# A hybrid decoder trunk on one core: constants, small tiles and pools padded so that large SBUF tiles lie at multiples of 256 bytes

## The chip, the cores and the metric

One core of one Trainium2 chip runs the kernel. The metric is device microseconds of one execution. The engines' names are those of the profile: PE (matrix multiply; PEld is its loading of weights), DVE, ACT, POOL (elementwise engines) and SP (which issues most DMAs). SBUF is the on-chip memory from which PE reads; an address in it is a byte offset that is the same in all 128 partitions.

## What is computed

A layer of three sub-layers on a residual stream x of 1024 tokens by 1024 features, all in float32:

```python
h = rms_norm(x, g[0]);  p = h @ w_in_first
y_conv = conformer_conv(p[..., :2 * D_CONV], ...)      # 31-tap causal convolution, layer norm, silu
y_rwkv, _ = rwkv7_mix(p[..., 2 * D_CONV:], ...)        # a recurrence over 1024 tokens, 8 heads of 64
x = x + rms_norm(concat([y_conv, y_rwkv]) @ w_out, g[1])
y = memory_cross_attention(rms_norm(x, g[2]), mem_n, wq, wkv, wo)   # 256 memory tokens, 4 heads
x = x + rms_norm(y, g[3])
y = swiglu(rms_norm(x, g[4]), w_gu, w_down)            # 1024 -> 2 x 2816 -> 1024
x = x + rms_norm(y, g[5])
```

## The kernel before

The 1024 tokens go in two blocks of 512. Every float32 product of a large matrix is made of three products of rounded parts (`mm3`, lines 192 to 196): each operand is split into a high part (`whi`, `ahi`, `fhi`: a rounding copy on ACT, line 166) and a low part (`wlo`, `alo`, `flo`: the difference, on DVE or POOL, line 167), and PE computes high by high (L194), high by low (L195) and low by high (L196). Weights come by DMA in tiles of 128 x 1024 floats (`wload`, lines 169 to 182), four raw buffers deep, two split buffers deep, four in the last feed-forward (pool `we`).

There are two forms. In `feat` (lines 198 to 206, output tile `psf`) a piece of 128 x 128 weights is the stationary operand and an activation tile of 128 x 512 is the moving one. In `tokmajor` (lines 208 to 227, output `pst`) 128 x 128 of an activation is stationary and 128 x 512 of weights is moving. Either way a weight tile gives 24 matmuls of 512 columns; the moving operand of one is 2048 contiguous bytes in each partition, the stationary one 512. By the code the 512-column matmuls of L194 to L196 are:

- input projection: 20 weight tiles of block 0 (activations in pool `a0`) and 22 of block 1 (pool `a1`), `feat`;
- output projection and the two products of attention, for each block 3 x 192, `tokmajor` (stationary in `a2` for block 0, `a3` for block 1);
- feed-forward of each block: gate and up, 44 weight tiles, `feat` (activations in `a2`, `a3`); down, 528 matmuls, `tokmajor` (stationary in `f0`, `f1`).

The order of work is fixed in `run` (line 946 on), partly by hand with generators that weave a side task into a main one: projections of block 0, preparation of the recurrence (`rwkv_prep`), triangular inverses (`rwkv_inverse`, lines 585 to 645, long on POOL), the chain over chunks (`rwkv_chain`) woven with the memory products and the convolution (`conv`, 31 taps a channel group on DVE); then output, attention, and the feed-forward of block 0 woven with the recurrence of block 1; at the end the feed-forward of block 1 alone. The framework's planner puts instructions on the engines' queues and lays out the tiles.

Where tiles lie: the planner rounds each buffer up to 32 bytes and stacks pools from both ends. The left stack starts at byte 16512 with the constants (`cols` 840 bytes, `lora_hi`, and so on), then pool `w` at 34880, `small` at 67648, and from 68480 the pools that are opened and closed on the left. The right stack starts at 229344 and grows downwards. Taken modulo 256, this puts the tiles of the constants at 224 or 64, all of `w` (`wraw`, `whi`, `wlo`) at 64, every large tile of a left pool (`a2`, `f0`, `f1`, `we`, `ya`) at 128, and every large tile of a right pool (`a0`, `a1`, `a3`, `mk`, `kv`) at 224. Buffers of 2080 bytes (tag `p2` of `rwkv_prep`) and 2168 bytes (`hin`) lie at changing multiples of 32.

Of the kernel before, what the change touches and what calls it, by code (L numbers as in the profile page):

```python
# [9 lines left out]
F32 = mybir.dt.float32  # L10
F32R = mybir.dt.float32r
# [6 lines left out]
P = 128  # L18
# [3 lines left out]
TB = 512  # L22
# [3 lines left out]
HP = 4  # L26
HEADS = 8
HD = 64
CH = 64
NCH = TB // CH  # L30
GW = 128
CONVW = 31
# [17 lines left out]
NCOLS = _o  # L50
# [19 lines left out]
class Trunk:  # L70
    def __init__(self, ctx, tc, x, mem, cols, lora, gpost, w_in, w_out, wqT, wkv, wo, w_gu, w_down, out):
        self.ctx, self.tc, self.nc = ctx, tc, tc.nc
        self.x, self.mem, self.out = x, mem, out
        self.w_in, self.w_out, self.wqT, self.wkv = w_in, w_out, wqT, wkv
        self.wo, self.w_gu, self.w_down = wo, w_gu, w_down
        self.gpost = gpost
        nc = self.nc
        pool = lambda name, bufs=1, **kw: ctx.enter_context(tc.tile_pool(name=name, bufs=bufs, **kw))
        self.cp = cp = pool("const")
        self.wp = self.wq = pool("w", 2)  # L80
        self.wbufs = 2
        self.sp = pool("small", 4)
        self.pd = pool("pd", 4, space=PSUM)
        self.pr = pool("pr", 3, space=PSUM)
        self.pn = pool("pn", 1, space=PSUM)
        dr = pool("dram", 1, space=DRAM)

        self.cols = cp.tile([P, NCOLS], F32, name="cols")
        nc.sync.dma_start(out=self.cols, in_=cols)
        self.lora = lora  # L90
        self.lora_hi = cp.tile([P, 3, DR], F32R, name="lora_hi")
        self.lora_lo = cp.tile([P, 2, DR], F32R, name="lora_lo")

        self.ident = cp.tile([P, P], F32, name="ident")
        make_identity(nc, self.ident)
        self.ones = cp.tile([P, P], F32, name="ones")
        nc.gpsimd.memset(self.ones, 1.0)
        self.mhalf = cp.tile([P, 1], F32, name="mhalf")
        nc.gpsimd.memset(self.mhalf, -0.5)
        self.carry = cp.tile([P, 14], F32, name="carry")  # L100
        nc.gpsimd.memset(self.carry, 0.0)
        self.smask = cp.tile([P, NCH, CH], F32, name="smask")
        nc.gpsimd.memset(self.smask, 1.0)
        nc.gpsimd.memset(self.smask[:, :, 0:1], 0.0)

        m = self.gmask = cp.tile([P, 2, 2 * CH], F32, name="gmask")
        nc.gpsimd.memset(m, 1.0)
        for r in (0, 1):
            rows = m[r * 64:(r + 1) * 64]
            for g in (0, 1):  # L110
                nc.gpsimd.affine_select(out=rows[:, g, 0:64], in_=rows[:, g, 0:64], pattern=[[1, 64]],
                                        compare_op=ALU.is_gt, fill=0.0, base=0, channel_multiplier=-1)
                nc.gpsimd.affine_select(out=rows[:, g, 64:128], in_=rows[:, g, 64:128], pattern=[[1, 64]],
                                        compare_op=ALU.is_ge, fill=0.0, base=0, channel_multiplier=-1)
            nc.vector.tensor_scalar(rows[:, r, 0:64], rows[:, r, 0:64], -1.0, None, op0=ALU.mult)


        def derive(name, n, src, mul, add):
            t = cp.tile([P, n], F32, name=name)
            nc.vector.tensor_scalar(t, src, mul, add, op0=ALU.mult, op1=ALU.add)  # L120
            return t
        col = self.col
        self.omu = derive("omu", 14, col("mu"), -1.0, 1.0)
        self.w0h = derive("w0h", 4, col("w0"), 0.5, 0.0)
        self.a0h = derive("a0h", 4, col("a0"), 0.5, 0.0)
        self.kah = derive("kah", 4, col("k_a"), 0.5, 0.0)
        self.kam = derive("kam", 4, col("k_a"), -0.5, 1.0)
        self.cwh = col("conv_w")
        nc.vector.tensor_scalar(self.cwh, self.cwh, 0.5, None, op0=ALU.mult)
        self.lgh = derive("lgh", 4, col("ln_g"), 0.5, 0.0)  # L130
        self.lbh = derive("lbh", 4, col("ln_b"), 0.5, 0.0)


        self.pool_share = self.share = 0.0
        self.state = cp.tile([P, HP, HD], F32, tag="state", bufs=2, name="state0")
        nc.gpsimd.memset(self.state, 0.0)
        self.blk = cp.tile([P, P], F32R, name="blk")
        nc.vector.tensor_copy(out=self.blk, in_=self.state[:, 0:2, :].rearrange("p h v -> p (h v)"))
        for i in (0, 64):
            nc.vector.tensor_copy(out=self.blk[i:i + 64, i:i + 64], in_=self.ones[i:i + 64, 0:64])  # L140

        self.hd = dr.tile([DR, CONVW - 1 + SEQ], F32, name="hd")
        self.pdr = dr.tile([14 * P, SEQ], F32, name="pdr")
        self.yd = dr.tile([D, SEQ], F32, name="yd")
        self.qd = dr.tile([DR, SEQ // CH, CH], F32, name="qd")
        self.amd = dr.tile([SEQ // CH, P, HEADS, 2 * CH], F32, name="amd")
        self.btd = dr.tile([SEQ // CH, P, HP, 2, HD], F32, name="btd")
        self.vtd = dr.tile([SEQ, DR], F32, name="vtd")
        self.bvd = dr.tile([DR, SEQ], F32, name="bvd")
        self.gnd = dr.tile([DR, SEQ], F32, name="gnd")  # L150
        self.gd = dr.tile([D, XH * MEM], F32, name="gd")
        self.vwd = dr.tile([XH * MEM, D], F32, name="vwd")
        self.x1d = dr.tile([SEQ, D], F32, name="x1d")
        self.x2d = dr.tile([SEQ, D], F32, name="x2d")
        NM = NCH * HEADS
        self.sc1 = [dr.tile([NM, CH, CH], F32, name=f"sc1_{i}") for i in range(NB)]
        self.sc2 = [dr.tile([2 * NM, 32, 32], F32, name=f"sc2_{i}") for i in range(NB)]
        self.sc3 = [dr.tile([NM, 32, 32], F32, name=f"sc3_{i}") for i in range(NB)]

    def col(self, name, i=None, n=1):  # L160
        a, b = COLS[name]
        return self.cols[:, a:b] if i is None else self.cols[:, a + i:a + i + n]
# [173 lines left out]
    def conv_taps(self, b, pool, acc):  # L336
        nc = self.nc
        t0 = b * TB
        for j in CONV_ORDER:
            h = pool.tile([P, TB + CONVW - 1], F32, tag="hin", bufs=2, name="hin")  # L340
            nc.sync.dma_start(out=h, in_=self.hd[j * P:(j + 1) * P, t0:t0 + TB + CONVW - 1])
            a = acc[:, j, :]
            w = lambda k: self.cwh[:, j * CONVW + k:j * CONVW + k + 1]
            nc.scalar.activation(out=a, in_=h[:, 0:TB], func=AF.Identity, scale=w(0), bias=self.col("conv_b", j))
            for k in range(1, CONVW):
                if j == CONV_POOL:
                    p = pool.tile([P, TB], F32, tag="t", bufs=2, name="tap")
                    nc.scalar.activation(out=p, in_=h[:, k:k + TB], func=AF.Copy, scale=w(k))  # L348
                    nc.gpsimd.tensor_tensor(out=a, in0=a, in1=p, op=ALU.add)  # L349
                else:  # L350
                    nc.vector.scalar_tensor_tensor(out=a, in0=h[:, k:k + TB], scalar=w(k), in1=a,  # L351
                                                   op0=ALU.mult, op1=ALU.add)
                if k % 6 == 0:
                    yield 4.0
# [62 lines left out]
    def rwkv_prep(self, b, pool):  # L417

        nc = self.nc
# [3 lines left out]
        half = (slice(0, 64), slice(64, 128))  # L423

        def flat2(name):
            t = pool.tile([P, NCH * (CH + 1)], F32, tag="p2", bufs=8, name=name)
            return t[:, 0:TB]

        def load(i, name):
            t = flat2(name)  # L430
            nc.sync.dma_start(out=t, in_=self.pdr[i * P:(i + 1) * P, t0:t0 + TB])
            return t
# [42 lines left out]
        def decays(hp):  # L475
# [4 lines left out]
            nc.vector.tensor_scalar(L, L, 1.0, None, op0=ALU.add)  # L480
            cs = flat2("cs")
            nc.vector.tensor_tensor_scan(cs, flat(self.smask), L, 0.0, op0=ALU.mult, op1=ALU.add)
            Dx = pool.tile([P, NCH, CH + 1], F32, tag="p2", bufs=8, name="Dx")
            nc.gpsimd.memset(Dx[:, :, 0:1], 1.0)
            nc.scalar.activation(out=Dx[:, :, 1:CH + 1], in_=c3(cs), func=AF.Exp, scale=-0.5 * DECAY)
            nc.scalar.activation(out=L, in_=cs, func=AF.Exp, scale=0.5 * DECAY)
# [463 lines left out]
    def run(self):  # L950
        tc = self.tc
        L, R = "left", "right"
        opened = {}

        def push(name, side):
            opened[name] = tc.tile_pool(name=name, bufs=1, side=side, reuse_waits="tile")
            return opened[name].__enter__()

        def pop(*names):
            for n in names:  # L960
                opened.pop(n).__exit__(None, None, None)
# [4 lines left out]
        self.credit = 0.0  # L966
        conv_cols, mix_cols = (4, 0, 6, 2), (20, 12, 8, 16, 14, 10, 18)

        a1 = push("a1", R)
        ev = push("ev", R)  # L970
        mk = push("mk", R)
# [79 lines left out]
        a3 = push("a3", R)  # L1051
        y1 = push("y1", R)
# [17 lines left out]
        pop("xe")  # L1070
        pop("we")
        pop("f1")
        pop("y1", "a3")


@with_exitstack
# [51 lines left out]
```

## Time and profile before

| | us |
|---|---|
| median of 3 runs (1662.28 to 1664.07) | 1663.06 |
| the profiled execution, whole | 1665.11 |
| its span, first to last instruction | 1663.4 |
| PE busy / DVE / ACT / POOL in the span | 1562.1 / 1055.0 / 722.0 / 368.7 |

PE is busy nearly all the time. Its matmuls are pipelined: the end of one is modelled, so the durations of single matmuls overlap, and the pace is read from starts, as the length of a stretch without waits divided by the weight loads in it, one for each matmul.

### The profile page before, as it was taken

Reading aid. Unit: us, or ns where it says so; the run is one execution under the profiler, and the core shown is the slowest. Engines: PE = TensorE matmul, PEld = TensorE weight load, DVE = VectorE, ACT = ScalarE, POOL = GpSimd, SP = SyncE. Lnnn points to the kernel's source line nnn. Section 1 sums busy time; section 2 is a strip of 40 time slices with the busy share of each in tenths; the row PEclk is TensorE's granted clock in tenths of the full one; section 3 lists DMA queues with packets and bytes.
Section 4 is the critical chain, followed back from the end, with each engine's and each line's share of the span. In section 5 each row is a group of like instructions: output and inputs, shape, how many; then the busy total and the mean of one; then the engine's idle time right before and its main releaser. Section 6 shows DMA issues by size and latency. Waiting matters only on the chain.

```text
span 1663.4 us, 22818 instructions
## 1 busy us (share of the span) xinstructions
PE 1562.1 (94%) x8688; PEld 1257.0 (76%) x8688; DVE 1055.0 (63%) x1501; ACT 722.0 (43%) x1122; POOL 368.7 (22%) x344
## 2 busy tenths in 40 slices
PE   7999866879999999999979889999999999999997
PEld 6777855767787888777757667777887788888886
DVE  5677698997545546768789996636537624343435
ACT  5654335867434434664224556524435232222222
POOL 1032390740000001022561730012113211111111
PEclk9999976889999999999999899999999999999999
DMA  6576967466636336457844335445236532323221
GB/s 206 166 223 190 283 203 220 127 196 216 234 117 203 95 100 192 139 165 210 252 119 141 96 114 161 157 126 204 87 91 229 214 102 89 102 89 101 89 89 51
DMA packets 175644, 257.37 MB, mean 155 GB/s; under 512 B 68912, under 2 KB 110000, under 8 KB 175536
## 3 DMA queue, kind: packets, MB, share of 16 engines
q1 hardware_dynamic: 174576, 255.08, 49.4%
q8 instruction: 68, 1.11, 0.3%
q10 hardware_dynamic: 960, 0.85, 0.2%
q14 instruction: 40, 0.33, 0.1%
HBM read 196.58 MB, written 59.31 MB: 154 GB/s over the span
## 4 chain that ended last, share of the span: by engine, by line
PE 46%; DVE 4%; POOL 4%; issue 2%; DMA 1%; ACT 0%; SPq 0%; POOLq 0%; DVEq 0%; ACTq 0%
PE psf L196 8%; PE psf L195 7%; PE psf L194 7%; PE pst L194 7%; PE pst L195 7%; PE pst L196 7%; DVE acc L351 2%; POOL Tt L617 1%; POOL tm L616 1%; PE psg L523 1%; DVE wlo L167 1%; DMA At<-sc 0%; PE pstr L274 0%; DMA btd<-bt 0%; POOL rstd L234 0%
## 5 line engine op out<-in xcount | busy, mean ns | idle before, releaser
L166 ACT CAST whi<-wraw 128x1024 fp32r<-128x1024 f32 x256 | 267.5, 1047 | 556.8 <-PE psf L195 222.7
L196 PE MATMUL psf<-ahi,wlo 128*128 128x512 f32 (+1 forms) x1200 | 468.7, 391 | 24.6 <-DVE wlo L167 23.5
L194 PE MATMUL psf<-ahi,whi 128*128 128x512 f32 (+1 forms) x1200 | 465.3, 389 | 9.6 <-ACT whi L166 9.4
L195 PE MATMUL psf<-alo,whi 128*128 128x512 f32 (+1 forms) x1200 | 465.1, 388 | 0.0
L167 DVE TENSOR_TENSOR wlo<-wraw,whi 128x1024 fp32r<-128x1024 f32 x223 | 284.7, 1278 | 268.4 <-ACT whi L166 266.7
L196 PEld LDWEIGHTS psf<-ahi,wlo 128*128 128x128 f32 x1200 | 232.3, 194 | 77.0 <-DVE wlo L167 29.2
L194 PEld LDWEIGHTS psf<-ahi,whi 128*128 128x128 f32 x1200 | 232.8, 194 | 58.8 <-ACT whi L166 11.8
L195 PEld LDWEIGHTS psf<-alo,whi 128*128 128x128 f32 x1200 | 232.9, 194 | 48.0 <-issue 1.2
L167 POOL TENSOR_TENSOR wlo<-wraw,whi 128x1024 fp32r<-128x1024 f32 x33 | 79.7, 2414 | 566.1 <-ACT whi L166 508.0
L351 DVE SCALAR_TENSOR_TENSOR acc<-hin,cols,acc 128x512 f32<-128x512 f32 x180 | 165.0, 945 | 0.7
L195 PE MATMUL pst<-wlo,ahi 128*128 128x512 f32 x384 | 152.2, 396 | 0.9 <-POOL wlo L167 0.9
L196 PE MATMUL pst<-whi,alo 128*128 128x512 f32 x384 | 150.5, 397 | 0.0
L194 PE MATMUL pst<-whi,ahi 128*128 128x512 f32 x384 | 137.3, 399 | 2.7 <-ACT ahi L277 2.1
L195 PE MATMUL pst<-wlo,fhi 128*128 128x512 f32 x352 | 138.8, 395 | 0.0
L196 PE MATMUL pst<-whi,flo 128*128 128x512 f32 x352 | 135.3, 393 | 0.0
L194 PE MATMUL pst<-whi,fhi 128*128 128x512 f32 x352 | 135.0, 396 | 0.0
L234 POOL TENSOR_TENSOR rstd<-rstd,mhalf 128x1 f32<-128x1 f32 x50 | 34.1, 689 | 394.1 <-DVE rstd L233 385.6
L349 POOL TENSOR_TENSOR acc<-acc,tap 128x512 f32<-128x512 f32 x60 | 97.1, 1618 | 87.5 <-ACT tap L348 84.1
L916 DVE TENSOR_TENSOR ya<-pst,ya 128x512 f32<-128x512 f32 x80 | 54.2, 686 | 53.5 <-PE pst L196 53.4
L194 PEld LDWEIGHTS pst<-whi,ahi 128*128 128x128 f32 x384 | 71.7, 188 | 20.1 <-ACT ahi L277 2.6
L195 PEld LDWEIGHTS pst<-wlo,ahi 128*128 128x128 f32 x384 | 72.1, 188 | 18.2 <-POOL wlo L167 1.2
L196 PEld LDWEIGHTS pst<-whi,alo 128*128 128x128 f32 x384 | 71.8, 188 | 16.6
(241 smaller groups left out, 2004.0 us busy)
## 6 DMA issues: line engine op xcount, KB each, us to landing
wraw<-in_w_gu_dram SPq DMA_DIRECT2D x88, 512.0 KB, 3.7
wraw<-in_w_in_dram SPq DMA_DIRECT2D x44, 512.0 KB, 4.5
wraw<-in_w_down_dram SPq DMA_DIRECT2D x44, 512.0 KB, 3.6
wraw<-in_wkv_dram SPq DMA_DIRECT2D x16, 512.0 KB, 5.4
am<-amd SPq DMA_DIRECT2D x16, 512.0 KB, 5.5
wraw<-in_w_out_dram SPq DMA_DIRECT2D x16, 512.0 KB, 4.1
wraw<-gd SPq DMA_DIRECT2D x16, 512.0 KB, 4.0
wraw<-vwd SPq DMA_DIRECT2D x16, 512.0 KB, 3.4
```

What stands on the lines that cost most here:

```text
L166: self.nc.scalar.copy(out=hi, in_=src)
L167: (eng or self.nc.vector).tensor_tensor(out=lo, in0=src, in1=hi.bitcast(F32), op=ALU.subtract)
L194: mm(ps, w[0], x[0], start=start, stop=False)
L195: mm(ps, w[0], x[1], start=False, stop=False)
L196: mm(ps, w[1], x[0], start=False, stop=stop)
L234: nc.gpsimd.tensor_tensor(r, r, self.mhalf, op=ALU.pow)
L349: nc.gpsimd.tensor_tensor(out=a, in0=a, in1=p, op=ALU.add)
L351: nc.vector.scalar_tensor_tensor(out=a, in0=h[:, k:k + TB], scalar=w(k), in1=a, op0=ALU.mult, op1=ALU.add)
L523: nc.tensor.matmul(pg[g][:, i, :], bk[half[g], c + i, :], aq[half[g], :, c + i, :], start=True, stop=True)
L616: eng.tensor_tensor(out=w, in0=a, in1=c, op=ALU.mult)
L617: eng.tensor_tensor(out=u, in0=u, in1=w, op=ALU.add)
L916: nc.vector.tensor_tensor(out=y, in0=ps, in1=y, op=ALU.add)
```

## The change

It alters where tiles lie and nothing that is computed. `cols` becomes 224 columns wide (896 bytes) of which 210 are used. The constants `state` and `blk` are made earlier, ahead of the small constants, `mhalf` and `carry` later, and a `pad` of 40 floats is added behind them. A tile `line` of 48 floats is added to the pool `small`, and a pool `edge` with one tile of 56 floats (224 bytes) is opened first on the right. Each of the three new tiles is set to zero once by POOL. `hin` and the buffers `p2` become 576 floats (2304 bytes) wide, of which the same columns as before are used.

```diff
+        nc.gpsimd.memset(self.sp.tile([P, 48], F32, tag="line", bufs=1, name="line"), 0.0)
...
-        self.cols = cp.tile([P, NCOLS], F32, name="cols")
+        self.cols = cp.tile([P, 224], F32, name="cols")[:, 0:NCOLS]
...
-        self.mhalf = cp.tile([P, 1], F32, name="mhalf")
-        nc.gpsimd.memset(self.mhalf, -0.5)
-        self.carry = cp.tile([P, 14], F32, name="carry")
-        nc.gpsimd.memset(self.carry, 0.0)
...
+        self.state = cp.tile([P, HP, HD], F32, tag="state", bufs=2, name="state0")
+        nc.gpsimd.memset(self.state, 0.0)
+        self.blk = cp.tile([P, P], F32R, name="blk")
+        nc.vector.tensor_copy(out=self.blk, in_=self.state[:, 0:2, :].rearrange("p h v -> p (h v)"))
+        for i in (0, 64):
+            nc.vector.tensor_copy(out=self.blk[i:i + 64, i:i + 64], in_=self.ones[i:i + 64, 0:64])
+        self.mhalf = cp.tile([P, 1], F32, name="mhalf")
+        nc.gpsimd.memset(self.mhalf, -0.5)
+        self.carry = cp.tile([P, 14], F32, name="carry")
+        nc.gpsimd.memset(self.carry, 0.0)
+        pad = cp.tile([P, 40], F32, name="pad")
+        nc.gpsimd.memset(pad, 0.0)
...
-            h = pool.tile([P, TB + CONVW - 1], F32, tag="hin", bufs=2, name="hin")
+            h = pool.tile([P, 576], F32, tag="hin", bufs=2, name="hin")[:, 0:TB + CONVW - 1]
...
-            t = pool.tile([P, NCH * (CH + 1)], F32, tag="p2", bufs=8, name=name)
+            t = pool.tile([P, 576], F32, tag="p2", bufs=8, name=name)
...
-            Dx = pool.tile([P, NCH, CH + 1], F32, tag="p2", bufs=8, name="Dx")
+            Dx = pool.tile([P, 576], F32, tag="p2", bufs=8, name="Dx")[:, 0:NCH * (CH + 1)].rearrange("p (c t) -> p c t", c=NCH)
...
+        edge = push("edge", R).tile([P, 56], F32, name="edge")
+        self.nc.gpsimd.memset(edge, 0.0)
...
-        pop("y1", "a3")
+        pop("y1", "a3", "edge")
```

## Rows read from the trace of the kernel before

**Rows 1.** The page: each engine's busy time, share of the span, instructions
```profile
PE 1562.1 (94%) x8688; PEld 1257.0 (76%) x8688; DVE 1055.0 (63%) x1501; ACT 722.0 (43%) x1122; POOL 368.7 (22%) x344
```

**Rows 2.** Windows: bounds, length, busy (x) of each engine, clock, DMA
```profile
200.00:300.00 100.00, 67.39 (x688) 56.66 (x686) 87.12 (x134) 46.10 (x79) 54.11 (x63) 0.74 0.70 220
300.00:400.00 100.00, 87.25 (x776) 74.64 (x777) 91.30 (x107) 68.78 (x111) 41.98 (x26) 0.90 0.59 189
400.00:500.00 100.00, 100.00 (x493) 79.72 (x493) 55.62 (x83) 49.15 (x74) 1.93 (x3) 1.00 0.52 169
...
900.00:1000.00 100.00, 87.01 (x598) 67.47 (x593) 93.50 (x105) 54.86 (x83) 49.30 (x30) 0.91 0.39 117
...
1100.00:1200.00 100.00, 99.16 (x451) 80.13 (x450) 50.07 (x84) 40.06 (x77) 17.03 (x13) 1.00 0.41 135
...
1500.00:1600.00 100.00, 100.00 (x434) 81.12 (x434) 39.88 (x45) 25.37 (x32) 12.01 (x5) 1.00 0.30 92
```

**Rows 3.** PE's waits, longest in total first: who, for whom, us, times, longest
```profile
PE psf L196 <- DVE wlo L167: 23.5, 13, 3.7
PE psvw L194 <- ACT whi L166: 12.1, 3, 5.8
...
PE psq L689 <- DVE Sn L706: 5.1, 4, 2.5
...
PE psv L577 <- DMA v<-pdr: 0.8, 1, 0.8
```

**Rows 4.** Windows without a wait, by place of operands; columns as in rows 2
```profile
42.06:56.58 14.52, 14.52 (x63) 11.68 (x62) 10.29 (x20) 9.00 (x15) 0.00 (x0) 1.00 0.68 201
...
692.45:712.14 19.69, 19.69 (x87) 16.15 (x86) 19.16 (x26) 10.17 (x16) 1.92 (x3) 1.00 0.42 109
1477.14:1521.95 44.81, 44.81 (x193) 36.04 (x192) 18.05 (x17) 11.94 (x16) 4.81 (x2) 1.00 0.35 106
450.36:494.46 44.10, 44.10 (x190) 35.53 (x189) 18.01 (x29) 15.05 (x26) 0.55 (x1) 1.00 0.43 140
1083.33:1127.43 44.10, 44.10 (x190) 35.48 (x189) 14.37 (x22) 12.04 (x21) 5.37 (x3) 1.00 0.39 119
1521.95:1543.75 21.80, 21.80 (x97) 18.02 (x96) 9.71 (x12) 4.73 (x5) 2.41 (x1) 1.00 0.25 79
```

**Rows 5.** Windows: matmuls of 256 columns at full clock, of 512 at half clock
```profile
362.82:368.04 5.22, 5.22 (x45) 5.20 (x44) 5.16 (x9) 2.71 (x4) 0.28 (x1) 1.00 0.75 223
256.08:261.62 5.54, 5.54 (x15) 4.29 (x13) 3.20 (x5) 0.99 (x2) 0.00 (x0) 0.51 1.09 260
```

**Rows 6.** Groups by line and shape: count, busy, mean ns, idle before
```profile
L167 DVE TENSOR_TENSOR wlo<-wraw,whi 128x1024 fp32r<-128x1024 f32 x223 | 284.7, 1278 | 268.4 <-ACT whi L166 266.7 <-ACT yq L691 1.0 <-DMA wraw<-in_w_in_dram 0.3
L166 ACT CAST whi<-wraw 128x1024 fp32r<-128x1024 f32 x256 | 267.5, 1047 | 556.8 <-PE psf L195 222.7 <-PE pst L196 193.7 <-issue 120.6
...
L499 DVE SCALAR_TENSOR_TENSOR ry<-cs,ry 128x512 f32<-128x512 f32 x8 | 5.5, 683 | 0.1
```

**Rows 7.** The same view: matmuls of 512 columns
```profile
L194 PE MATMUL psf<-ahi,whi 128*128 128x512 f32 x1040 | 414.8, 400 | 6.7 <-ACT whi L166 6.7
...
L194 PE MATMUL pst<-whi,ahi 128*128 128x512 f32 x384 | 137.3, 399 | 2.7 <-ACT ahi L277 2.1 <-DVE ya L916 0.5
...
L194 PE MATMUL pst<-whi,fhi 128*128 128x512 f32 x352 | 135.0, 396 | 0.0
```

**Rows 8.** Timeline of the start: start, us, engine, line, what
```profile
1.12 0.11 POOL L101 MEMSET carry<- 128x14 f32 x1
...
2.22 0.31 POOL L136 MEMSET state<- 128x256 f32 x1
...
6.20 0.15 DVE L233 TENSOR_SCALAR rstd<-ss 128x1 f32<-128x1 f32 x1 [1.66 <-ACT junk L248]
6.51 0.55 POOL L234 TENSOR_TENSOR rstd<-rstd,mhalf 128x1 f32<-128x1 f32 x1 [2.18 <-DVE rstd L233]
```

**Rows 9.** The chain that ended last, in order of time
```profile
803.55 7.01 DMA At<-sc
```

More of the change, by code (lines that the diff above doesn't have):

```diff
@@ L134, in __init__ @@
         self.pool_share = self.share = 0.0
[L135 to L140, printed above, removed]
         self.hd = dr.tile([DR, CONVW - 1 + SEQ], F32, name="hd")
```

## Prediction

> **What bounds the kernel now.** I read the page's first section, then stretches of 100 us, then PE's waits. PE is busy for 94% of the span, DVE for 63% [rows 1]. From 400 to 700 us and from 1100 to 1600 us PE is full or within 3% of it at full clock, with DVE at 39 to 61 us of 100 (eight stretches, three of them shown); only between 200 and 400 us and between 800 and 1000 us does PE idle, drop to half clock and meet DVE at 87 to 93 us of 100 [rows 2]. Its waits are few: the largest is 23.5 us in 13 pieces for `wlo` from DVE, and for a DMA 0.8 us is the longest entry [rows 3]. So the end is set by the pace of PE's own matmuls. The duration in a row of groups (400 ns) is no pace, since ends are modelled. The pace is read from stretches in which nothing waits: length divided by the weight loads in it.
>
> **What the pace depends on.** Addresses are not in the trace. They follow from the stacks of tiles as described above, and I give them as the remainder modulo 256 of moving, then stationary operand. The six stretches of 512-column matmuls [rows 4], in their order:
> - `a0` moving, `w` stationary, (224, 64): 14.52 / 62 = 234.2 ns (`a1`, later, lies the same)
> - `a2`, `w`, (128, 64): 19.69 / 86 = 229.0
> - `a3`, `we`, (224, 128): 44.81 / 192 = 233.4
> - `w`, `a2`, (64, 128): 44.10 / 189 = 233.3
> - `w`, `a3`, (64, 224): 44.10 / 189 = 233.3
> - `we`, `f1`, (128, 128): 21.80 / 96 = 227.1
>
> The comparison is close to an experiment. The first three run the same code (`feat`) and differ in where the operands lie; the last three run the same code (`tokmajor`). A moving operand at 128 costs 5 to 6 ns less than one at 64 or 224, and between these two there is no difference; a stationary one at 128 is worth 1 or 2 ns more. It isn't load from other engines: in the 229.0 stretch DVE is busy 19.16 of 19.69 us, and in the 233.4 stretch 18.05 of 44.81.
> At half clock 13 matmuls at (64, 224) take 5.54 us, 426 ns each, and half of that is 213 [rows 5]: there the 512 columns alone set the pace, at one column a cycle of 1.2 GHz. At full clock 256 columns at (224, 64) take 5.22 / 44 = 118.6 ns [rows 5]; twice that less 234.2 leaves 3.0 ns that don't grow with columns. So without any loss per column a matmul would take 213.3 + 3.0 = 216.3 ns, and the rest, 17.9 ns at (224, 64) and 10.8 at (128, 128), grows with the bytes that are streamed and depends on the address.
>
> **Part 1, matmul operands.** The sum of sizes after the change: constants end at 35072 instead of 34880, `w` at 67840, `small` at 68864, and the right stack begins at 229120. All four are multiples of 256, and so is the size of every large buffer, so every operand of L194 to L196 goes to (0, 0). The code has 5328 such matmuls of 512 columns, three times 1040 + 384 + 352 [rows 7]. By class: 1008 at 234.2, 1056 at 229.0, 1056 at 233.4, 1104 at 233.3 (all of block 0's `tokmajor`), 576 at 233.3, 528 at 227.1.
> No operand of the trace is at 0, so the new pace has to be bounded. From above by the nearest row, 227.1: 7.2 + 2.0 + 6.7 + 6.8 + 3.6 + 0 = 26.2 us saved. From below by 216.3: another 10.8 x 5328 = 57.5 us. Past the upper end lies 234, if 0 were as bad as 64 (rival 2). I take 224.4. It is halfway between the nearest row and the middle of the two bounds (221.7): going from 64 to 128 took off 6 to 7 of 17.9 ns, and a further step of that kind down to 0 is as likely as none. That saves 26.2 + 2.7 x 5328 = 40.6 us.
> Not all reaches the end. By the starts in the timeline, 93% of these matmuls follow the one before at full clock and within 250 ns; the others run at half clock or behind a wait and gain nothing. Some 11% of the 93% lie in 300 to 400 and 800 to 1000 us, where DVE and POOL's inverses are late next; there I count half. 40.6 x 0.88 = 35.7 us. The 672 matmuls of 256 columns (by the code: the first panel and the memory products) gain half as much each, 4.9 ns, 3.3 us, and lie where PE is not the bound for about half their time: 1.5 us. Sum 37.2 us.
>
> **Part 2, elementwise engines.** Nothing. L499 reads `cs` at 0, 32, 64, 96, 160 and 192 in its eight instances and `ry` at 128 and 224; its mean is 683 ns for 512 columns, and a weight split takes 1278 ns for 1024, at 64. The ACT split takes 1047 ns over 256 instances, at 64 in `w` and at 128 in `we` [rows 6]. Even a gain would be hidden: ACT and DVE prepare a weight tile in 1.05 and 1.28 us while PE spends 24 x 0.23 = 5.6 us on one.
>
> **Part 3, what is added and moved.** Three POOL memsets of 40 to 56 columns cost between 0.11 us (14 columns) and 0.31 us (256 columns) [rows 8], say 0.13 each. POOL has been idle for 2.18 us when the first `rstd` comes, and that waits for ACT's sum by way of DVE [rows 8]. Cost 0; 0.4 us without that cover. Queued behind them are POOL's constants, which the first projections don't need. The three `blk` copies go ahead of DVE's small constants; DVE then still has most of the 1.66 us before its first `rstd` [rows 8]. Memsetting `state` earlier in the program can't hold up the one DMA on ACT's queue that reads it; if the planner put it behind POOL's masks instead, which end at 6.51 - 2.18 = 4.33 us, ACT would start up to 2 us later. I take 0, since it now runs at 2.22 us, in front of them, and its place in the program only moves forward.
> The larger `p2` buffers make `rwkv_prep` 1792 bytes bigger. It still ends at 136448 below `a0` at 136960, so no pool waits for another that it didn't wait for; on the left, `Tt` of the inverse now also covers the old `ry`. Its memset then waits for readers that finish before the 7.01 us load of `At`, which the same loop needs [rows 9]. Cost 0. DMA counts and sizes stay.
> The planner may place a few instructions differently. PE's largest single waits are 3.7 to 5.8 us [rows 3], so I allow 6 us either way for that.
>
> **Total.** 1663.1 - 37.2 = 1625.9 against the median. Against the profiled execution's 1665.1 it is 1628; that one lies 2 us above the median, and the difference carries over.
>
> **Rivals.**
> 1. All of the loss per column goes. Pace 216.3: (26.2 + 57.5) x 0.88 + 3.0 = 76.7 us, time 1586. For it: the half-clock row shows that columns alone can set the pace. Against it: the step to 128 removed only a third of the loss. The Trainium skill, "TensorE: Matmul & The Clock Gate", section "Back-to-back issue gap", gives a gap of N/2.4 + 2.5 ns, 216 ns at 512 columns, whatever the address. No stretch in this trace reaches it; by that figure 1586 would be what full alignment gives back.
> 2. Slower: 0 behaves like 64 and 224, and 128 was the good place, for instance because both operands then start on the same phase. It decides as soon as (0, 0) costs over 232 ns, today's average. At 234.2 the classes at (128, 64) and (128, 128) lose 5.2 x 1056 + 7.1 x 528 = 9.2 us, the others 2.4 us; x 0.88 = 10 us, time 1673. For it: cost is not monotonic in the remainder (224 is as bad as 64). Against: 64 and 224 share that they are no multiples of 128, and 0 is one.
> 3. Nothing changes, 1663: alignment beyond the 32 bytes that every tile has doesn't count, and the differences in pace come from the stage. The Trainium skill, "SBUF — State Buffer", section "Specifications (TRN2)", names lines of 16 bytes as what access is sensitive to; by that rule all these tiles are equal already. The trace disagrees with it for PE: 227.1 against 233.3 ns in the same code.
> 4. PE gets faster but the end doesn't follow: waits for `wlo` (23.5 us now) grow, or a changed order adds stalls, so that under 15 us are left. Time 1650 to 1660. Against: in the eight full stretches DVE has 40 us of 100 to spare [rows 2].
>
> **How the numbers follow.** Forecast (pace 221.7 to 227.1, time 1612 to 1639) 0.70; rival 1 0.12; rival 2 0.07; rival 3 0.05; rival 4 0.06. Range 1586 to 1656: it takes in the forecast with the planner's 6 us, the near half of rival 1 and the near half of rival 4, and leaves out 0.06 below and 0.15 above. About 0.2% (3.3 us) is what a measurement of this kernel can tell from no change. Faster: 0.70 + 0.12 + 0.05 of rival 4 = 0.87; the same: 0.05 (rival 3) + 0.01 of rival 4 = 0.06; slower: 0.07 (rival 2).
>
> **What would show it.** The feed-forward of block 1 from 1300 us on is the test: its `feat` stretches should fall from 233.4 ns and its `tokmajor` stretches from 227.1 to one and the same pace. At 227 only the row is confirmed and the time is near 1639; at 222, 1612; at 216, rival 1; at 233 or more, rival 2. At half clock 426 ns should stay. DVE and ACT means should not move. I am wrong if the pace falls and PE's waits grow by as much.

## The result and the profile after

| | before | after |
|---|---|---|
| median, us (lowest to highest, 4 runs each) | 1662.67 (1661.02 to 1664.07) | 1641.54 (1637.86 to 1643.87) |
| the profiled execution, its span | 1665.11, 1663.4 | 1639.46, 1637.7 |

The ratio is 0.9871 with a 95% interval of 0.9847 to 0.9895: 21 us less, where 37 were forecast (1626, range 1586 to 1656). The profiled executions lie 2 us above the one median and 2 us below the other, so between the traces 25.7 us are to be found.

The page of after, first section (busy us, share of the span, instructions):

```profile
PE 1537.0 (94%) x8688; PEld 1256.5 (77%) x8688; DVE 1056.9 (65%) x1501; ACT 721.7 (44%) x1122; POOL 369.3 (23%) x347
```

Against [rows 1] PE lost 25.1 us of busy time; the other engines moved by less than 2 us. The three instructions more are POOL's memsets. Apart from these and the constants at the start, which moved on DVE and POOL as in the diff, every engine issues the same instructions in the same order. The tiles lie where the sum of sizes put them: each large one at a multiple of 256.

Windows of after: the six stretches of [rows 4] in the same order, then two that answer to [rows 5], 256 columns at full clock and 512 at half clock (bounds, length, busy (x) of PE, PEld, DVE, ACT, POOL, clock, DMA share, GB/s):

```profile
42.16:56.25 14.09, 14.09 (x63) 11.64 (x62) 10.12 (x18) 9.10 (x15) 0.00 (x0) 1.00 0.69 213
680.15:699.70 19.55, 19.55 (x87) 16.14 (x86) 19.01 (x25) 10.03 (x15) 1.91 (x3) 1.00 0.36 108
1454.88:1498.41 43.53, 43.53 (x193) 36.04 (x193) 18.03 (x17) 11.95 (x15) 4.79 (x2) 1.00 0.35 109
443.54:486.43 42.89, 42.89 (x190) 35.44 (x189) 17.97 (x29) 15.11 (x26) 0.55 (x1) 1.00 0.44 144
1068.87:1111.76 42.89, 42.89 (x190) 35.47 (x189) 14.35 (x22) 12.08 (x21) 5.33 (x3) 1.00 0.39 123
1498.41:1520.17 21.76, 21.76 (x97) 18.02 (x96) 9.71 (x12) 4.73 (x5) 2.39 (x1) 1.00 0.27 81
356.73:361.97 5.24, 5.24 (x45) 5.20 (x44) 5.18 (x9) 2.72 (x4) 0.73 (x1) 1.00 0.75 231
252.18:254.31 2.13, 2.13 (x7) 1.65 (x5) 2.13 (x4) 0.00 (x0) 0.00 (x0) 0.50 1.17 190
```

Length over the matmuls that start in it (62, 86, 192, 189, 189, 96; the third window also counts a load that runs over its edge): 227.3, 227.3, 226.7, 226.9, 226.9 and 226.7 ns. The six paces have become one. The 256-column stretch gives 5.24 / 44 = 119.1 ns (118.6 in [rows 5]): no gain. At half clock it is 2.13 / 5 = 426 ns, as before. Over the some 5,080 matmuls of 512 columns that follow the one before at full clock, the mean from start to start fell from 232.1 to 227.35 ns; that is 24 us, nearly all of the difference.

The same stretches show when it was gained. Their starts moved by 0 (42 us), 6.8 (450), 12.3 (692), 14.5 (1083), 22.3 (1477) and 23.5 us (1522), and the end by 25.7. Between 692 and 1083 us, where block 1's recurrence runs beside the feed-forward of block 0, only 2.2 us came. There was little to gain there: by their starts the 512-column matmuls of this stretch lost 3.1 us, since most are of the class at (128, 64), which stood at 229.0 already.

PE's waits of after (who, for whom, us, times, longest), then three groups (count, busy, mean ns, idle before), then the start of POOL and DVE (start, us, engine, line, what); line numbers are five higher than before from the constants on:

```profile
PE psf L201 <- DVE wlo L172: 25.1, 15, 4.1
PE psvw L199 <- ACT whi L171: 11.7, 3, 6.0
...
PE psq L694 <- DVE Sn L711: 5.3, 4, 2.5
```

```profile
L172 DVE TENSOR_TENSOR wlo<-wraw,whi 128x1024 fp32r<-128x1024 f32 x223 | 285.9, 1283 | 253.4 <-ACT whi L171 251.9 <-ACT yq L696 0.6 <-DMA wraw<-in_w_in_dram 0.3
L171 ACT CAST whi<-wraw 128x1024 fp32r<-128x1024 f32 x256 | 268.0, 1049 | 533.8 <-PE psf L200 182.6 <-PE pst L201 182.1 <-issue 153.7
...
L504 DVE SCALAR_TENSOR_TENSOR ry<-cs,ry 128x512 f32<-128x512 f32 x8 | 5.5, 683 | 0.1
```

```profile
0.80 0.14 POOL L83 MEMSET line<- 128x48 f32 x1 [0.29 <-POOLq L1123]
...
2.54 0.13 POOL L128 MEMSET pad<- 128x40 f32 x1
2.61 0.14 POOL L975 MEMSET edge<- 128x56 f32 x1
...
6.20 0.15 DVE L238 TENSOR_SCALAR rstd<-ss 128x1 f32<-128x1 f32 x1 [1.51 <-ACT junk L253]
6.50 0.55 POOL L239 TENSOR_TENSOR rstd<-rstd,mhalf 128x1 f32<-128x1 f32 x1 [1.93 <-DVE rstd L238]
```

The waits of [rows 3] stand nearly as they were (`wlo` 23.5 to 25.1 us). The splits and the in-place product of [rows 6] take what they took. The added memsets come out of POOL's idle time, and the first `rstd` starts at 6.20 us as in [rows 8].

### The profile page after: what moved, and what is told of

Same layout as the page of the kernel before. It is cut to its first block, busy times and chain, and to the rows that moved or that the text cites. A ratio compares the mean times of both kernels' runs of the same rounds, so it can differ in the third digit from the quotient of the medians.

```text
span 1637.7 us, 22825 instructions
## 1 busy us (share of the span) xinstructions
PE 1537.0 (94%) x8688; PEld 1256.5 (77%) x8688; DVE 1056.9 (65%) x1501; ACT 721.7 (44%) x1122; POOL 369.3 (23%) x347
## 4 chain that ended last, share of the span: by engine, by line
PE 44%; DVE 5%; POOL 4%; issue 2%; DMA 1%; ACT 1%; SPq 0%; POOLq 0%; DVEq 0%; ACTq 0%
PE psf L201 7%; PE psf L199 7%; PE psf L200 7%; PE pst L199 6%; PE pst L200 6%; PE pst L201 6%; DVE acc L356 2%; POOL tm L621 1%; POOL Tt L622 1%; DVE wlo L172 1%; PE psg L528 1%; DMA At<-sc 0%; DVE ya L921 0%; POOL rstd L239 0%; POOL wlo L172 0%
## 5 line engine op out<-in xcount | busy, mean ns | idle before, releaser
L171 ACT CAST whi<-wraw 128x1024 fp32r<-128x1024 f32 x256 | 268.0, 1049 | 533.8 <-PE psf L200 182.6
L201 PE MATMUL psf<-ahi,wlo 128*128 128x512 f32 (+1 forms) x1200 | 462.6, 386 | 26.2 <-DVE wlo L172 25.1
L200 PE MATMUL psf<-alo,whi 128*128 128x512 f32 (+1 forms) x1200 | 460.3, 384 | 0.0
L172 DVE TENSOR_TENSOR wlo<-wraw,whi 128x1024 fp32r<-128x1024 f32 x223 | 285.9, 1283 | 253.4 <-ACT whi L171 251.9
L201 PEld LDWEIGHTS psf<-ahi,wlo 128*128 128x128 f32 x1200 | 231.5, 193 | 74.7 <-DVE wlo L172 30.3
L199 PEld LDWEIGHTS psf<-ahi,whi 128*128 128x128 f32 x1200 | 231.7, 193 | 53.0 <-ACT whi L171 10.0
L200 PEld LDWEIGHTS psf<-alo,whi 128*128 128x128 f32 x1200 | 231.8, 193 | 42.7 <-issue 1.2
L201 PE MATMUL pst<-whi,alo 128*128 128x512 f32 x384 | 148.4, 391 | 0.0
L201 PE MATMUL pst<-whi,flo 128*128 128x512 f32 x352 | 134.3, 390 | 0.0
L354 POOL TENSOR_TENSOR acc<-acc,tap 128x512 f32<-128x512 f32 x60 | 99.4, 1656 | 85.6 <-ACT tap L353 82.0
L201 PEld LDWEIGHTS pst<-whi,alo 128*128 128x128 f32 x384 | 71.8, 188 | 14.5
```

Source lines behind the costliest of these rows:

```text
L171: self.nc.scalar.copy(out=hi, in_=src)
L172: (eng or self.nc.vector).tensor_tensor(out=lo, in0=src, in1=hi.bitcast(F32), op=ALU.subtract)
L199: mm(ps, w[0], x[0], start=start, stop=False)
L200: mm(ps, w[0], x[1], start=False, stop=False)
L201: mm(ps, w[1], x[0], start=False, stop=stop)
```

## The experiments

What is left to ask is why the pace fell, since that decides what another kernel should do. Three theories come first. A is the prediction's: the place of the moving operand counts, and multiples of 128 are the good ones. B: it has to be a multiple of 256. C: only the place of the moving operand relative to the stationary one counts, modulo 256, and equal places are the best. The six rows of before fit C as well as A: moving less stationary is 160, 64, 96, 192, 96 and 0, and the paces are 234.2, 229.0, 233.4, 233.3, 233.3 and 227.1. Places are given as (moving, stationary) modulo 256.

**All tiles at 128, all tiles at 64.** From after, both pads altered alike:

```diff
-        pad = cp.tile([P, 40], F32, name="pad")
+        pad = cp.tile([P, 72], F32, name="pad")      # all128; 56 in all64
...
-        edge = push("edge", R).tile([P, 56], F32, name="edge")
+        edge = push("edge", R).tile([P, 88], F32, name="edge")      # all128; 40 in all64
```

> The changed kernel with both stacks shifted so that every large tile lies at 128 modulo 256 (constants stay at 0). Theory A (what counts is a multiple of 128): pace of the 512-column matmuls 227 ns in every stretch, time within 5 us of the changed kernel, about 1641. Theory B (256 itself counts, and a part of the gain comes from it): pace 229 or more, time 1648 or more. Theory C (what counts is that both operands start at the same place modulo 256): 227 ns, 1641, as A.

> The changed kernel with both stacks shifted so that every large tile lies at 64 modulo 256. Theory A (multiples of 128): pace 233 to 235 ns everywhere, 7 ns over the changed kernel; 7.3 x 5328 x 0.88 = 34 us more, about 1675, which is 10 us above the kernel before, where a third of the operands lay at 128. Theory C (same place for both): 227 ns, about 1641. A line of 16 bytes: no difference, 1641.

Measured: all128 1642.87 us (1641.02 to 1646.9), ratio 0.9877 [0.9859, 0.9894]; all64 1646.51 us (1646.4 to 1647.85), 0.9898 [0.9881, 0.9914]. Windows of all64, `a3` over `we`, `w` over `a2`, `we` over `f1`:

```profile
1461.94:1505.47 43.53, 43.53 (x193) 36.06 (x192) 18.03 (x17) 11.94 (x16) 4.78 (x2) 1.00 0.36 109
447.25:490.14 42.89, 42.89 (x190) 35.47 (x189) 17.96 (x29) 14.87 (x26) 0.55 (x1) 1.00 0.45 144
1505.47:1527.23 21.76, 21.76 (x97) 18.03 (x96) 9.71 (x12) 4.73 (x5) 2.39 (x1) 1.00 0.25 82
```

These are after's lengths to the hundredth, at a place that A holds to be as bad as any. A falls, B with it; C holds. The time of all64 is 5 us above after's at the same pace; its stretches begin 3.7 us late at 443 us and 7.1 us late at 1455 us, so the loss lies outside the dense stretches: over all its 512-column matmuls at full clock the mean is 227.4 ns, after's 227.3. What it is was not found; the intervals of the two ratios overlap.

**The right stack alone, the left stack alone.** right_only is before with only the `edge` tile: `a0`, `a1`, `a3` go to 0, the left stack stays. left_only is after without it: the left goes to 0, the right stays at 224.

```diff
+        edge = push("edge", R).tile([P, 56], F32, name="edge")      # right_only, added to before
+        self.nc.gpsimd.memset(edge, 0.0)
...
-        pop("y1", "a3")
+        pop("y1", "a3", "edge")
...
-        edge = push("edge", R).tile([P, 56], F32, name="edge")      # left_only, taken from after
-        self.nc.gpsimd.memset(edge, 0.0)
...
-        pop("y1", "a3", "edge")
+        pop("y1", "a3")
```

> The kernel before with the pool edge alone, so that the pools of the right stack (a0, a1, a3, mk, kv) go from 224 to 0 and everything else stays. Theory A: a0 and a1 as moving operand over w at 64 fall from 234.2 to 229, a3 over we at 128 from 233.4 to 227; 5.2 x 1008 + 6.4 x 1056 = 12 us, x 0.9 = 11 us, about 1652. tokmajor with w as moving operand stays at 233. Theory C (same place for both): a3 at 0 over we at 128 would not gain, about 1660.

> The changed kernel without the pool edge: constants, w, small and the left pools at 0, the right pools stay at 224. Theory A: w as moving operand falls from 233 to 227 (stationary at 0) or 228 (stationary at 224), a2 from 229 to 227, a0, a1, a3 stay at 233 to 234; 6.5 x 1104 + 5 x 576 + 2.3 x 1056 = 12.5 us, x 0.9 = 11 us, about 1652. With right_only the two halves should add up to the whole, 21 to 25 us.

Measured: right_only 1660.46 us (1657.61 to 1665.25), ratio 0.998 [0.9968, 0.9992]; left_only 1658.36 us (1655.56 to 1660.42), 0.9969 [0.9955, 0.9982]. Windows of right_only, `a3` over `we` (0, 128), `w` over `a3` (64, 0), then `a2` over `w` (128, 64) twice:

```profile
1472.63:1517.43 44.80, 44.80 (x193) 36.04 (x192) 18.07 (x17) 11.96 (x16) 4.81 (x2) 1.00 0.35 106
1081.32:1124.58 43.26, 43.26 (x190) 35.51 (x189) 14.34 (x22) 12.03 (x21) 5.36 (x3) 1.00 0.38 122
691.29:711.35 20.06, 20.06 (x87) 16.26 (x86) 19.53 (x26) 10.28 (x15) 2.09 (x4) 1.00 0.38 110
668.12:679.11 10.99, 10.99 (x49) 9.02 (x48) 7.25 (x10) 6.94 (x12) 0.00 (x0) 1.00 0.63 178
```

and of left_only, `a3` over `we` (224, 0), `w` over `a2` (0, 0):

```profile
1471.94:1516.74 44.80, 44.80 (x193) 36.08 (x192) 18.06 (x17) 11.96 (x16) 4.80 (x2) 1.00 0.35 106
447.58:490.46 42.88, 42.88 (x190) 35.47 (x189) 17.96 (x29) 14.84 (x25) 0.55 (x1) 1.00 0.44 144
```

A moving operand at 0 over a stationary one at 128, both multiples of 128, costs 44.80 / 192 = 233.3 ns: no gain at all, where A had the best pace. (64, 0) gives 228.9 ns; in before the same code at (64, 224) had 233.3. So it is 64 bytes ahead that is worth 4 ns, and not a place. In left_only the pace falls to 226.9 ns just where both operands are on the left. The halves save 3 and 5 us, the whole 21: the gain belongs to the pair. The paces say the same: the mean over all 512-column matmuls at full clock is 232.1 ns in before, 231.5 in right_only, 230.4 in left_only and 227.3 in after. Of left_only's 1.7 ns, 8.5 us in all, only 5 reached the end.

One row doesn't fit: the third of right_only has 233.3 ns at (128, 64), where 229.0 was due. The fourth row is the same class in the same run some 20 us earlier, and has 10.99 / 48 = 229.0; over all 950 matmuls of the class the mean is 229.9. The starts show how they differ. In the dense rows at 64 ahead three matmuls in turn take 226, 229 and 232 ns, though all three have the same places, and which product gets which changes from run to run (in before L194 226.0, L195 229.1, L196 231.7; in off64, below, the first product 231.8, the second 226.0, the third 229.1). In the odd row all three take 233 to 234. So the difference of places fixes the pace of most stretches but not of each matmul, and at 64 ahead PE can also run slow for a stretch. Why was not settled.

**A scan of places.** From after, in the feed-forward of block 1 the split weight tiles (`whi`, `wlo`) start 0, 4, 8 ... 224 bytes into larger buffers, a new place for each weight tile:

```diff
...
+        if self.wbufs == 4:
+            at = self.places[k].pop(0)
+            self.places[k].append(at)
+            hi, lo = (self.wq.tile([P, 1088], F32R, tag=t, bufs=4, name=t)[:, at:at + 1024]
+                      .rearrange("p (k n) -> p k n", k=k) for t in ("whi", "wlo"))
...
```

> The changed kernel, in the feed-forward of block 1 with the split weight tiles of pool we made 1088 floats wide and each one started 0, 4, 8, 16, 32, 64, 96, 128, 160, 192 or 224 bytes into its buffer in turn; all else at 0. In the down products they are moving operands, in gate and up stationary ones. Theory A (multiples of 128): as moving operand 227 ns at 0 and 128, 232 to 234 at all the others alike; as stationary one 227 at 0 and 128 and 228 to 229 at the others. A line of 16 bytes: 227 at 0, 16, 32 and all multiples, more at 4 and 8 alone. A line of 32 or 64 bytes is excluded already.

Measured: one run, 1650.58 us. Windows of 24 matmuls in scan, stationary weights at 0, 4, 64, 192 and 224 under a moving `a3` at 0, then moving weights at 0 and 4 over a stationary `f1` at 0:

```profile
1344.92:1350.37 5.45, 5.45 (x25) 4.51 (x24) 0.69 (x1) 1.54 (x2) 2.39 (x1) 1.00 0.15 38
1350.37:1355.95 5.58, 5.58 (x25) 4.51 (x24) 2.52 (x3) 1.57 (x2) 0.00 (x0) 1.00 0.45 153
...
1394.97:1400.56 5.59, 5.59 (x25) 4.52 (x24) 1.92 (x2) 1.05 (x1) 0.00 (x0) 1.00 0.46 166
...
1417.35:1422.85 5.50, 5.50 (x25) 4.51 (x24) 2.76 (x2) 1.57 (x2) 2.00 (x1) 1.00 0.24 57
1422.85:1428.44 5.59, 5.59 (x25) 4.50 (x24) 1.82 (x2) 1.54 (x2) 0.00 (x0) 1.00 0.40 131
...
1317.07:1322.52 5.45, 5.45 (x25) 4.51 (x24) 2.51 (x3) 3.34 (x5) 0.00 (x0) 1.00 0.33 99
1322.52:1328.22 5.70, 5.70 (x25) 4.55 (x24) 1.23 (x1) 3.19 (x5) 0.00 (x0) 1.00 0.27 78
```

Mean from start to start, in ns, by the place of the weights, over some 90 matmuls each where they are stationary and 48 to 72 where they move; the other operand lies at 0:

| place of the weights | 0 | 4 | 8 | 16 | 32 | 64 | 96 | 128 | 160 | 192 | 224 |
|---|---|---|---|---|---|---|---|---|---|---|---|
| stationary | 227.0 (tiles without a wait) | 232.4 | 230.4 | 233.1 | 233.1 | 233.2 | 233.8 | 232.1 | 233.4 | 229.4 | 233.2 |
| moving | 227.8 | 237.3 | 233.4 | 231.7 | 233.1 | 229.8 | 233.7 | 233.0 | 233.7 | 232.6 | 232.6 |

Only equal places give 227. A second, half-good case is the moving operand 64 ahead: stationary at 192 (229.4), moving at 64 (229.8). All else costs 230 to 237, 4 bytes included. With these two cases the table gives back all six rows of before: 64 ahead 229.0, equal 227.1, the differences 96, 160 and 192 between 233.3 and 234.2.

**A test of that table.** off64 is after with `edge` at 40 floats: the right stack at 64, the left at 0. By C with the scan's table (C2 in the expectation), `a0`, `a1` and `a3` are 64 ahead of the stationary operand where they move; where they are stationary, the moving one is 64 behind. off256 has `edge` at 120 floats, so that right and left differ by 256 modulo 512.

```diff
-        edge = push("edge", R).tile([P, 56], F32, name="edge")
+        edge = push("edge", R).tile([P, 40], F32, name="edge")      # off64; 120 in off256
```

> The changed kernel with the right stack 64 bytes further, so that a0, a1, a3, mk and kv lie at 64 modulo 256 and w, we, a2, f0, f1 at 0. Theory C2 (only moving less stationary place modulo 256 counts: 227 ns at a difference of 0, 229 at 64, 233 at 192), from the runs so far: a0 and a1 over w and a3 over we at 229 to 230, w over a3 in tokmajor at 233, a2 over w, w over a2 and f0, we over f1 at 227. Against the kernel before 4.8 x 1008 + 4 x 1056 + 1.7 x 1056 + 6.1 x 1104 = 17.6 us, x 0.9 = 16 us less, about 1648. Theory A (multiples of 128, place of the moving operand): a0, a1, a3 at 233, w over a3 at 228.

> The changed kernel with the right stack 256 bytes further down, so that a0, a1, a3 lie at 0 modulo 512 and w, we, a2, f0, f1 at 256 modulo 512; in the changed kernel all lie at 256 modulo 512. Theory C2 with a period of 256 bytes: 227 ns everywhere, time as the changed kernel, about 1641. Theory C2 with a period of 512 or more: a0, a1, a3 over w and we and w over a3 at 232 to 234, about 1655.

Measured: off64 1651.6 us (1646.62 to 1655.29), ratio 0.9911 [0.9888, 0.9935]; off256 1642.8 us (1641.18 to 1647.19), 0.9873 [0.9856, 0.9889]. Windows of off64, then of off256, each `a3` over `we` and `w` over `a3`:

```profile
1469.43:1513.40 43.97, 43.97 (x193) 36.06 (x192) 18.05 (x17) 11.96 (x16) 4.81 (x2) 1.00 0.34 108
1080.11:1124.21 44.10, 44.10 (x190) 35.34 (x189) 14.39 (x22) 12.16 (x22) 5.34 (x3) 1.00 0.39 119
```

```profile
1457.85:1501.38 43.53, 43.53 (x193) 36.05 (x192) 18.03 (x17) 11.96 (x16) 4.79 (x2) 1.00 0.36 109
1071.84:1114.69 42.85, 42.85 (x190) 35.47 (x189) 14.31 (x22) 12.09 (x21) 5.34 (x3) 1.00 0.40 124
```

43.97 / 192 = 229.0 with the moving operand 64 ahead, 44.10 / 189 = 233.3 with it 64 behind: the table held, and it depends on the sign. The time expected for off64, about 1648, was missed by 3.6 us; its four runs spread over 8.7. At a difference of 256 both stretches have 226.7, as at 0, so the period is 256 bytes.

**Is the rest a cost per column?** widths_0 is after with the gate and up products of block 1 made in pieces of 512, then 256, then 128 columns; widths_224 is the same from left_only, so that the moving `a3` lies at 224.

```diff
-                pg = self.feat(self.wcols(self.w_gu, f), hT, TB)
+                parts = 1 if self.wbufs == 2 or f < 8 else 2 if f < 16 else 4
+                pg = self.feat(self.wcols(self.w_gu, f), hT, TB, parts)
...
```

> The changed kernel, in the feed-forward of block 1 with gate and up of weight tiles 8 to 15 in two matmuls of 256 columns and of 16 to 21 in four of 128. Operands at 0. Theory P (the loss left at 0 is per column, as the prediction split it): 213.3 + 13.4 at 512, 106.7 + 7 to 8 = 114 at 256, 53.3 + 5 = 58 at 128. Theory F (a fixed 13 ns for each matmul): 227, 120, 66. Theory L (the loading of the 128 x 128 weights sets a floor under short matmuls): 227, 118 to 120, and no less than 110 at 128 columns.

> The same widths with the right stack left at 224, so that the moving operand a3 lies at 224 and the weights at 0. Theory P: 233 at 512, 118 at 256 (4 more than at 0), 61 at 128. Theory F: 233, 123, 68. Theory L: 233 at 512, and at 256 and 128 columns the same as at 0, because the moving operand isn't what a short matmul waits for.

Measured: one run each, 1712.4 and 1720.76 us. Windows of 512, 256 and 128 columns in widths_0, then in widths_224:

```profile
1328.63:1372.19 43.56, 43.56 (x194) 36.06 (x193) 14.33 (x15) 12.45 (x17) 7.18 (x3) 1.00 0.31 100
1393.91:1440.02 46.11, 46.11 (x386) 46.07 (x385) 16.27 (x17) 11.93 (x15) 4.81 (x2) 1.00 0.31 102
1540.00:1552.20 12.20, 12.20 (x112) 12.20 (x111) 2.51 (x3) 2.61 (x4) 0.00 (x0) 1.00 0.14 44
```

```profile
1336.87:1381.70 44.83, 44.83 (x193) 36.07 (x192) 14.34 (x15) 12.47 (x17) 7.21 (x3) 1.00 0.30 97
1403.46:1448.93 45.47, 45.47 (x385) 45.44 (x384) 16.28 (x17) 11.94 (x15) 4.80 (x2) 1.00 0.31 103
1545.00:1557.20 12.20, 12.20 (x112) 12.20 (x111) 1.82 (x2) 1.54 (x2) 0.00 (x0) 1.00 0.15 44
```

From start to start these are 226.7, 120.0 and 111.6 ns at equal places, 233.3, 118.3 and 111.6 at 224 over 0 (the windows also count matmuls that run over an edge). At equal places 512 columns take 106.7 ns more than 256, which is what 256 columns take at 2.4 GHz. What lies above the columns is then 13.4 ns at 512 (226.7 less 213.3) and 13.3 at 256 (120.0 less 106.7). That is what a fixed cost would give (theory F of the expectation), but it isn't shown to be one: F's 66 ns at 128 columns did not come, and theory L, a floor set by the weight loads, expected 118 to 120 and no less than 110 and fits all three widths. The rows of the loads can't part the two, because each lasts about 190 ns, they overlap, and they fill the stretch at 256 columns (46.07 of 46.11 us) as they do at 128 (12.20 of 12.20). Theory P's 114 ns at 256 didn't come either; if the loads set the 120.0, that doesn't rule out a loss per column at 512. Places 224 over 0 add 6.6 ns at 512 columns, take off 1.7 at 256 and change nothing at 128.

**The wider buffers.** narrow is after with `p2` and `hin` at their old widths (2080 and 2168 bytes).

```diff
...
-            t = pool.tile([P, 576], F32, tag="p2", bufs=8, name=name)
+            t = pool.tile([P, NCH * (CH + 1)], F32, tag="p2", bufs=8, name=name)
...
```

> The changed kernel with the buffers p2 and hin at their old widths, 2080 and 2168 bytes; all other tiles stay at 0. The padding of these two touches operands of DVE, ACT and POOL and DMA targets alone. Theory A, PE's operands alone count: same time as the changed kernel, about 1641, DVE and ACT means unchanged. Rival: DVE or DMA gained from it: 1645 or more.

Measured: 1642.2 us (1639.72 to 1644.41), ratio 0.987 [0.9847, 0.9893], after's. These buffers hold no operand of the dense matmuls, and their padding does nothing that can be seen.

**Which stationary tile counts?** While a matmul streams, the next weights are loaded. lo128 is after with `wlo` of the last feed-forward at 128 and all else at 0, so that every third matmul loads, and every third uses, a tile out of step, that is at another place than its stream.

```diff
+        at = 32 if self.wbufs == 4 else 0
+        lo = self.wq.tile([P, 1024 + 2 * at], F32R, tag="wlo", bufs=self.wbufs, name="wlo")[:, at:at + 1024]
...
```

> The changed kernel, in the feed-forward of block 1 with the tiles wlo of pool we at 128 and whi, a3 and f1 at 0. In feat the three matmuls of a step are L199 (whi stationary, ahi moving), L200 (whi, alo), L203 (wlo, ahi; last line of mm3). Theory N (a matmul is slowed by the load of the NEXT one's weights, which runs beside it): the middle one, beside which wlo is loaded, takes 232 and the other two 227. Theory O (by the place of its OWN weights): the last one takes 232. Theory V (average over the stream): all three at 228 to 229.

Measured: one run, 1645.62 us. The timeline of PE there (start, us, line, what; L201 to L203 are the three products):

```profile
1458.36 0.39 PE L201 MATMUL psf<-ahi,whi 128*128 128x512 f32 x1
1458.58 0.40 PE L202 MATMUL psf<-alo,whi 128*128 128x512 f32 x1
1458.82 0.40 PE L203 MATMUL psf<-ahi,wlo 128*128 128x512 f32 x1
1459.05 0.39 PE L201 MATMUL psf<-ahi,whi 128*128 128x512 f32 x1
```

Over some 350 matmuls of each kind, from a start to the next: L201 226.8, L202 232.4, L203 234.1 ns. L201 uses `whi` and loads `whi` next; L202 uses `whi` and loads `wlo`; L203 uses `wlo` and loads `whi`. So neither theory N (only the load counts) nor O (only its own tile counts) is enough alone: the matmul beside which the out-of-step tile is loaded is slow, and so is the one that uses it. In `tokmajor`, with `wlo` moving, only that one matmul is slow (234.1; the others 225.9 and 226.6).

The scan bears on both halves where the place changes from one weight tile to the next. At its three dense changes from 0 to 4, the last matmul of the old tile, in step itself but with the new tile loaded beside it, takes 235 or 236 ns after 227: the load counts. At its three dense changes from 224 to 0, the last matmul of the old tile, out of step but with a load in step beside it, takes 226, 226 and 232. So that the matmul which uses an out-of-step tile is slow holds for lo128 and not in general; there it may also carry over from the slow matmul before it, which no run tests. What in PE's reading makes it so stays open.

## Why the prediction was right, and where it was off

**What bounds the kernel: right.** PE's pace set the end. 24 us of pace were removed and 25.7 us of span went with them; PE's waits hardly grew (25.1 us for `wlo` after 23.5), so rival 4 did not come.

**What the pace depends on: the wrong reading of the right rows.** The prediction took the moving operand's place for the cause and gave the stationary one 1 or 2 ns. (128, 128) was the best row of [rows 4] because the two were equal, and (128, 64) the second because it is 64 ahead; right_only (233.3 ns at (0, 128)) and all64 (226.7 at (64, 64)) show that 128 has no part in it. The change puts all operands at one place, so both readings say that it helps; only the experiments part them. That the time fell at all was to that extent luck: right_only moves `a3` to a multiple of 128, as the prediction's reading wants, and `a3` over `we` stays at 233.3. Six rows in which both places vary together can't tell a place from a difference; that was to be seen before, and should have been a rival of its own.

**Part 1: the term that was too large.** The step "3.0 ns that don't grow with columns, and the rest grows with the bytes" compared two widths at (224, 64), where 256 columns pay nothing for their places and 512 pay 6 to 7 ns. At equal places 13.4 ns stay above the columns and no pace below 226.7 was found, so the halfway value 224.4 was not to be had. With the measured paces, 226.7 to 227.3, the prediction's classes give 26.8 us instead of 40.6, by its 0.88 23.6 instead of 35.7, and the 256-column term of 1.5 is 0: 1639.5 us. That is the 1639 that it named for "only the row is confirmed", and 2 us from the median, within the spread of after's runs. The factor 0.88 did well in the sum. Its reason, gains lost where DVE and POOL are late next, is roughly borne out: from 346 to 450 us 0.7 us of the 1.6 that the matmuls' starts gave came, and from 692 to 1083 us 2.2 of 3.1.

**Parts 2 and 3: right at nothing.** DVE's split has 1283 ns (1278), ACT's 1049 (1047), L504 683 (683). The memsets cost 0.13 to 0.14 us each, in idle time; narrow shows the same for the wider buffers. The planner's order didn't change.

**The rivals.** Rival 1 wanted 216.3; at 512 columns no pace shown here is below 225.9. The Trainium skill, "TensorE: Matmul & The Clock Gate", section "Back-to-back issue gap", has a fixed part of 2.5 ns. These runs show 13.4 above the columns at the best places, so its 216 ns were not reached by placement. Rival 2 expected (0, 0) to cost 232 ns or more; it costs 226.7 to 227.3. Both operands starting on the same phase, which it named in passing, is what the best rows share. Rival 3 is out by all the runs. The Trainium skill, "SBUF — State Buffer", section "Specifications (TRN2)", names lines of 16 bytes. They don't explain the scan, where 16 and 32 bytes cost 4 to 6 ns, as much as most other places do.

## What to carry to other kernels

Where dense matmuls of 512 float32 columns set the time, put the tiles that are streamed and those that are loaded as weights at the same address modulo 256 bytes; which address doesn't matter, and aligning half of the tiles gives little (3 and 5 us of 21 here). Read the pace from starts, and compare rows by the difference of the two places before blaming either. Products of 256 and 128 columns gained nothing from it here (224 over 0 against equal places).

## What the runs showed of the hardware

- The pace of a 512-column matmul depends on moving less stationary place modulo 256: 226.7 ns at 0, 229 at 64 (but 233.3 in one stretch of right_only), 230 to 237 at the other differences tried. It isn't symmetric: 64 behind costs 233.3 (off64).
- The worst place tried is the smallest step: weights moving 4 bytes off take 237.3 ns (scan).
- At 64 ahead three matmuls in turn take 226, 229 and 232 ns with the same places, so only a mean over many is a pace.
- At 256 columns 224 over 0 is slightly faster than equal places (118.3 against 120.0 ns), and at 128 columns both take 111.6 ns.
- A stationary tile out of step slows the matmul during which it is loaded (232.4 ns in lo128, 235 or 236 in the scan). The one that uses it was slow in lo128 (234.1) and fast in two of three cases of the scan (226). No run shows why.
